# The woven SwiGLU of one encoder layer: main units in another order, and the convolution's weights transposed later

## The chip, the cores and the metric

One core of a Trainium2 chip (trn2) computes one layer of an encoder. The metric is the device time of one execution in microseconds, lower is better. Engines in this text: PE (matrix products), PEld (its weight loads), DVE and ACT (elementwise work), POOL, and SP (issues most loads).

## What is computed

All weights are float32, there are 256 rows of 2048 channels. Cut to what matters here:

```python
def _swiglu(x, w1, w3, w2):
    return (jax.nn.silu(x @ w1) * (x @ w3)) @ w2      # w1, w3: 2048 x 5632, w2: 5632 x 2048

x = _layer_norm(ALPHA * x + 0.5 * _swiglu(x, ffn1_w1, ffn1_w3, ffn1_w2), ln1_g, ln1_b)
mix = _hybrid_mixer(x, w_in, b_gates_m, conv_m, ...)  # begins with x @ w_in and a causal convolution
x = _layer_norm(ALPHA * x + mix, ln2_g, ln2_b)
x = _layer_norm(ALPHA * x + 0.5 * _swiglu(x, ffn2_w1, ffn2_w3, ffn2_w2), ln3_g, ln3_b)
x = x + jax.nn.sigmoid(x @ w_ple_gate) * (p @ w_ple_proj)
```

So there are two feed-forward networks (FFNs) of the same shape, with a mixer between them. The hidden width 5632 is 11 chunks of 512 columns, chunk 0 to 10.

## The kernel before

**Units.** The program for PE is a list of `Unit`s, written out by hand and walked from front to back (line 1043). A unit multiplies one weight tile of 256 rows by 512 columns with one half of the rows (128 rows, `tt` 0 or 1). Each float32 operand is split in two parts, hi and lo, so a unit is two k-steps of three products (lines 1061 to 1063), six in all. A weight tile is loaded on SP (line 983, `raw`), split by ACT (line 1010, hi) and by DVE (line 1014, lo), some tiles ahead of PE. Raw tiles, splits, transposed activations and wide temporaries share one pool of 44 buffers, and `loads` (line 976) issues the next load only while the count of activation buffers (`pages[0]`) and raw tiles leaves room.

**One FFN** (`ffn`, line 424) has 496 units:

- `up(c)`: for the chunks 0, 5 and 8, a gate part (x @ w1, 16 units, then Silu on ACT into a temporary `temp`) and a hidden part (x @ w3, 16 units, then a multiplication on DVE, line 442).
- `up7(c)`: for the other eight chunks gate and hidden together in a scheme of seven products (`seven`, line 314): 28 units, with sums of weights made by accumulating loads on POOL (line 330) and by DVE (line 335). Its last product is number 3; after it DVE multiplies gate and hidden for the first half of the rows (line 473), and `late` does so for the second half (line 484).
- `down(*chunks)`: the hidden chunk times w2 in four groups of 512 output columns. `down(c)` is 16 units, four for each group, two for each half; each group and half has a PSUM bank of its own, which DVE adds into the residual `xres` (line 497). `down(4, 5)` takes two chunks into one bank: 32 units with half as many additions.

Before a chunk goes into `down`, it must be transposed: `transposed` (line 263) makes four PE transposes of 128 x 128 (line 266), a copy on ACT (line 268) and a subtraction on DVE (line 274), which give the two parts of `actT` (here called hT).

**The order.** `main` is a list of parts of `up` and `down`; `chained` strings the eight `up7` chunks together (order 1, 2, 3, 4, 6, 7, 9, 10) with pauses (`None`) where a chunk waits for its sums; `weave` spreads this side list evenly over main, from main's ninth unit on. `down(9)` and `down(10)` stand behind the woven part.

**When the rest is issued.** A small planner (`Sched`) holds the steps that come later than the unit that causes them. Its clock advances by 6 x 0.2161 us a unit (line 1064), and a step is issued when it is due: a chunk is turned `DELAY["h"]` = 8 us after its multiplication, for the second half of a woven chunk `DELAY["late"]` = 9 us + 8 us after product 3, and turns are kept 3.4 us apart. If a unit needs a chunk that isn't transposed yet, the planner runs what it holds until it is:

```python
        sched.until(lambda: u.act.ready(u.chunk, u.tt))      # line 1049
```

The transposes then stand in the program right ahead of the unit that reads them.

**The convolution's weights.** `mixer_setup` (line 533) is called once, ahead of `down(9)` of the first FFN. It loads the convolution's weights (line 539) behind what SP has queued, and spawns `later` (line 547), which, 4 us on by the planner's clock, transposes them on PE (line 550) and copies them on DVE (line 551). `conv` (line 653) needs them; it follows the first group of the mixer (`head`, 16 units).

Of the kernel before, what the change touches and what calls it, by code (L numbers as in the profile page):

```python
# [156 lines left out]
def weave(main, side):  # L157

    n = sum(isinstance(u, Unit) for u in main)
    out, at, seen = [], 0, 0  # L160
    for u in main:
        out.append(u)
        if isinstance(u, Unit):
            seen += 1
            while at < len(side) and at * n < seen * len(side):
                if side[at] is not None:
                    out.append(side[at])
                at += 1
    return out


def flat(pairs):
    return [u for p in pairs for u in p]


def skewed(pairs):
    return [p[0] for p in pairs] + [p[1] for p in pairs]
# [3 lines left out]
def kernel(  # L181
# [25 lines left out]
    def temp():  # L207
        sched.until(lambda: temps[0] < TEMP_BUFS)
        temps[0] += 1
        return temp_pool.tile([P, COL], F32, name="temp", tag="temp")  # L210

    def drop(n=1):
        temps[0] -= n

    def misc(shape):
        return ps_pool.tile(shape, F32, name="ms", tag="ps")
# [19 lines left out]
    def activate(out, in_, func, **kw):  # L236
        use_table(func)
        nc.scalar.activation(out, in_, func, **kw)  # L238
# [24 lines left out]
    def transposed(src, act, c, t):  # L263
        ps = misc([P, 4, P])
        for k in range(4):
            nc.tensor.transpose(ps[:, k], src[:, k * P:(k + 1) * P], ident[:])  # L266
        dst = act.get(c, t)
        nc.scalar.copy(dst[:, 0], ps[:])  # L268
        if act.forms:
            if c not in act.whole:  # L270
                act.whole[c] = big()
                pages[0] += 1
            nc.scalar.copy(act.whole[c][:, t * COL:(t + 1) * COL], ps.rearrange("q k s -> q (k s)"))
        nc.vector.tensor_tensor(out=dst[:, 1], in0=ps[:], in1=dst[:, 0], op=ALU.subtract)  # L274
        act.mark(c, t, 4)
        if act.forms and all(act.ready(c, h) for h in range(TT)):
            sched.spawn(form_turn(act, c), DELAY["form"] + 3.0 * c)
# [26 lines left out]
    def group(w, rows, col0, cols, act, done):  # L304

        accs = [{} for _ in range(TT)]
        pairs = []
        for i, r in enumerate(rows):
            tile = plain(rows_of(w, r, col0, cols))
            pairs.append([Unit(tile, t, accs[t], act, r // COL, r % COL // P,  # L310
                               i == 0, i == len(rows) - 1, done) for t in range(TT)])
        return pairs
# [58 lines left out]
    def boundary(mixer):  # L371
        program.append(Boundary(mixer))
# [51 lines left out]
    def ffn(w1, w3, w2, act, norm, skew=True, ahead=()):  # L424
        n = FF // COL
        hT = ActT(act_tile)

        def turn(src, c, t):
            transposed(src, hT, c, t)
            drop()  # L430
            return
            yield

        def up(c):
            s = {}

            def gate(ps, t):
                s[t] = temp()
                activate(s[t][:], ps, ACT.Silu)

            def hidden(ps, t):
                nc.vector.tensor_tensor(out=s[t][:], in0=ps, in1=s[t][:], op=ALU.mult)
                sched.spaced(turn(s[t], c, t), DELAY["h"] + 2.0 * t, TURN_GAP)

            return group(w1, range(0, D, 2 * P), c * COL, COL, act, gate), group(w3, range(0, D, 2 * P), c * COL, COL, act, hidden)

        def up7(c):
            s = {}

            def both(out, a, b, op):  # L450
                nc.vector.tensor_tensor(out=out, in0=a, in1=b, op=op)

            def done(m, banks):
                ps = {k: v["ps"][:] for k, v in banks.items() if v}
                if m == 5:
                    e = temp()
                    nc.scalar.copy(e[:], ps["E"])
                    banks["B"]["ps"], banks["W"]["ps"] = seeded
                    both(banks["B"]["ps"][:], ps["X"], e[:], ALU.subtract)
                    drop()  # L460
                elif m == 6:
                    nc.scalar.copy(banks["W"]["ps"][:], ps["B"])
                elif m == 4:
                    s[1] = temp()
                    nc.scalar.copy(s[1][:], ps["E"])
                elif m == 2:
                    s[0] = temp()
                    sched.spawn(silu(s[0], ps["X"]), DELAY["silu"])
                elif m == 7:
                    both(s[1][:], ps["W"], s[1][:], ALU.add)  # L470
                    sched.spawn(silu(s[1], s[1][:]), DELAY["silu"])
                elif m == 3:
                    nc.vector.scalar_tensor_tensor(out=s[0][:], in0=ps["B"], scalar=-1.0, in1=s[0][:],
                                                   op0=ALU.mult, op1=ALU.mult)
                    sched.spaced(turn(s[0], c, 0), DELAY["h"], TURN_GAP)
                    sched.spawn(late(ps["W"]), DELAY["late"])

            def silu(out, src):
                activate(out[:], src, ACT.Silu)
                return  # L480
                yield

            def late(w):
                nc.vector.scalar_tensor_tensor(out=s[1][:], in0=w, scalar=-1.0, in1=s[1][:],
                                               op0=ALU.mult, op1=ALU.mult)
                sched.spaced(turn(s[1], c, 1), DELAY["h"], TURN_GAP)
                return
                yield

            return seven(w1, w3, D, c * COL, COL, act, done)  # L490

        def down(*chunks):
            pairs = []
            for g in range(D // COL):
                def add(ps, t, g=g):
                    xs = xres[t][:, g * COL:(g + 1) * COL]
                    nc.vector.scalar_tensor_tensor(out=xs, in0=ps, scalar=0.5, in1=xs,  # L497
                                                   op0=ALU.mult, op1=ALU.add)
                    if n - 1 in chunks:
                        norm.chunk(t, g)  # L500
                pairs += group(w2, [c * COL + r for c in chunks for r in (0, 2 * P)], g * COL, COL, hT, add)
            return pairs

        gate, hidden = zip(*(up(c) for c in (0, 5, 8)))
        program.extend((skewed(gate[0][:SKEW]) if skew else flat(gate[0][:SKEW])) + flat(gate[0][SKEW:]))
        rest, tail = down(9), down(10)
        main = flat(hidden[0] + gate[1] + down(0) + down(1) + hidden[1] + down(2) + down(3) + gate[2] + down(4, 5) + hidden[2] + down(6)
                    + down(7, 8))
        program.extend(main[:8] + weave(main[8:], chained([up7(c) for c in (1, 2, 3, 4, 6, 7, 9, 10)])))
        program.append(norm.load)  # L510
        program.extend(ahead)
        program.extend(flat(rest) + flat(tail[:-SKEW]) + skewed(tail[-SKEW:]))
        boundary(True)
# [19 lines left out]
    def mixer_setup():  # L533
        st["sel"] = big()[0:HM, 0:HM * P].rearrange("q (h s) -> q h s", s=P)
        nc.vector.memset(st["sel"], 1.0)
        nc.gpsimd.affine_select(st["sel"], st["sel"], pattern=[[-1, HM], [0, P]], compare_op=ALU.is_equal,
                                fill=0.0, base=0, channel_multiplier=1)
        raw = temp()
        nc.sync.dma_start(out=raw[0:64, 0:P], in_=conv_m[0].rearrange("j (b q) -> (j b) q", q=P))
        st["cw"] = small.tile([P, 64], F32, name="cw", bufs=1)  # L540
        st["bi"] = small.tile([HM, 1], F32, name="bi", bufs=1)
        st["bf"] = small.tile([HM, 1], F32, name="bf", bufs=1)
        bg = b_gates_m[0].rearrange("(a h) -> a h", h=HM)
        nc.sync.dma_start(out=st["bi"][:], in_=bg[0].rearrange("(h o) -> h o", o=1))
        nc.sync.dma_start(out=st["bf"][:], in_=bg[1].rearrange("(h o) -> h o", o=1))

        def later():
            yield 4.0
            ps = misc([P, 64])
            nc.tensor.transpose(ps[:], raw[0:64, 0:P], ident[0:64, 0:64])  # L550
            nc.vector.tensor_copy(out=st["cw"][:], in_=ps[:])
            drop()
            flags.add("cw")
        sched.spawn(later())
# [546 lines left out]
```

## Time and profile before

| | |
|---|---|
| three timed runs | 2250.76, 2250.98, 2256.62 us, median 2250.98 |
| the profiled execution, its own time | 2255.85 us |
| its span, first to last instruction | 2254.1 us |
| share of the span in which PE is busy | 98% |
| DVE, ACT, POOL | 75%, 55%, 9% |
| mean granted clock of PE | 0.993 |
| read from HBM | 497.91 MB, 222 GB/s over the span with what is written |

The first FFN takes the first 730 us or so, the mixer the time to about 1430 us, the second FFN the time to about 2155 us. In views of instructions a row names the line, engine and operation, then what is written and read, a count, busy us and the mean ns of one. In the waits a row says who stood idle, for whom, how long in total, how often, and the longest. A row of windows gives for each engine its busy us and in brackets the number of instructions, then the granted clock of PE (1.00 is full), the DMA engines' share and GB/s. The names in such rows are the program's: `mm` is a product's PSUM bank, `ms` the bank of a transpose, `temp` a temporary that holds a hidden chunk, `split` a split weight.

### The profile page before, as it was taken

The page shows a single profiled execution, that of the slowest core. Times are in us where ns is not written, and L with a number is a line of the kernel's source. Part 1 is how long each engine was busy: PE and PEld are TensorE (multiplying, and loading weights), DVE is VectorE, ACT ScalarE, POOL GpSimd, SP SyncE. Part 2 cuts the span into 40 slices and gives each one's busy share as a digit, 9 for nine tenths or more (in the row PEclk, how much of TensorE's full clock was granted, in tenths as well). Part 3 has the DMA queues.
Part 4 walks back from the last instruction along what each step waited for, and adds up shares of the span by engine and source line. Part 5 has one row for each costly group of instructions (what it writes and reads, how often), then busy time and mean ns, then how long its engine had stood idle before and what let it go on. Part 6 is the DMA issues. An engine that isn't in the chain of part 4 may idle for free. (4 is left out here: it accounts for less than half of the span.)

```text
span 2254.1 us, 27470 instructions
## 1 busy us (share of the span) xinstructions
PE 2213.1 (98%) x10065; PEld 1828.4 (81%) x10065; DVE 1682.6 (75%) x1840; ACT 1237.8 (55%) x1441; POOL 201.9 (9%) x175
## 2 busy tenths in 40 slices
PE   9999999999998999999999999999999999999999
PEld 7878877888887888888888888788787878888878
DVE  6889987888898765654555456788888878889873
ACT  6556655556573555545653344456565666666552
POOL 3111001011100000100100000121011110100000
PEclk9999999999999999999999999999999999999999
DMA  9899779897992665565566666679878979989542
GB/s 344 220 251 298 219 217 271 236 260 216 293 339 81 201 188 159 177 182 148 174 181 186 194 221 218 224 177 283 239 233 227 293 214 273 265 252 296 203 158 95
DMA packets 262856, 501.83 MB, mean 223 GB/s; under 512 B 15744, under 2 KB 24768, under 8 KB 262720
## 3 DMA queue, kind: packets, MB, share of 16 engines
q1 hardware_dynamic: 227904, 432.95, 58.3%
q0 software_dynamic: 34816, 67.12, 16.6%
q8 instruction: 79, 1.29, 0.2%
q14 instruction: 57, 0.47, 0.1%
HBM read 497.91 MB, written 2.10 MB: 222 GB/s over the span
## 5 line engine op out<-in xcount | busy, mean ns | idle before, releaser
L1014 DVE TENSOR_TENSOR split<-raw,split 128x1024 fp32r<-128x1024 f32 (+1 forms) x1013 | 1183.0, 1203 | 331.7 <-ACT split L1010 298.0
L1010 ACT CAST split<-raw 128x1024 fp32r<-128x1024 f32 (+1 forms) x1013 | 1018.6, 1038 | 450.6 <-PE mm L1062 104.8
L1061 PE MATMUL mm<-split,actT 128*128 128x512 f32 (+2 forms) x2768 | 1081.1, 391 | 9.3 <-ACT actT L268 8.8
L1063 PE MATMUL mm<-split,actT 128*128 128x512 f32 (+2 forms) x2768 | 1070.3, 387 | 10.6 <-DVE actT L274 10.6
L1062 PE MATMUL mm<-split,actT 128*128 128x512 f32 (+2 forms) x2768 | 1069.1, 386 | 2.6 <-DVE split L1014 2.6
L1063 PEld LDWEIGHTS mm<-split,actT 128*128 128x128 f32 x2768 | 522.7, 189 | 122.2 <-DVE actT L274 17.4
L1061 PEld LDWEIGHTS mm<-split,actT 128*128 128x128 f32 x2768 | 523.0, 189 | 112.9 <-ACT actT L268 10.7
L1062 PEld LDWEIGHTS mm<-split,actT 128*128 128x128 f32 x2768 | 523.3, 189 | 104.0 <-DVE split L1014 3.7
L330 POOL DMA_DIRECT2D raw<-in_ffn_w_dram x128 | 155.6, 1221 | 1013.2 <-DVE split L1014 823.7
L335 DVE TENSOR_TENSOR raw<-raw 128x1024 f32<-128x1024 f32 x128 | 155.7, 1217 | 11.5 <-DMA raw<-in_ffn_w_dram 11.5
L1061 PE MATMUL seeded<-split,actT 128*128 128x512 f32 x384 | 150.4, 392 | 0.0
L1063 PE MATMUL seeded<-split,actT 128*128 128x512 f32 x384 | 150.0, 391 | 0.0
L1062 PE MATMUL seeded<-split,actT 128*128 128x512 f32 x384 | 150.0, 391 | 0.0
L268 ACT CAST actT<-ms 128x512 fp32r<-128x512 f32 x84 | 49.1, 589 | 131.4 <-PE ms L266 131.2
L497 DVE SCALAR_TENSOR_TENSOR xres<-mm,xres 128x512 f32<-128x512 f32 x144 | 97.9, 683 | 21.4 <-PE mm L1063 21.4
L1061 PEld LDWEIGHTS seeded<-split,actT 128*128 128x128 f32 x384 | 72.4, 189 | 15.0
L1063 PEld LDWEIGHTS seeded<-split,actT 128*128 128x128 f32 x384 | 72.4, 188 | 15.1
L1062 PEld LDWEIGHTS seeded<-split,actT 128*128 128x128 f32 x384 | 72.4, 189 | 15.1
L274 DVE TENSOR_TENSOR actT<-ms,actT 128x512 fp32r<-128x512 f32 x84 | 57.1, 684 | 30.1 <-ACT actT L268 18.9
L421 POOL TENSOR_SCALAR xres<-xres 128x512 f32<-128x512 f32 x16 | 27.5, 1724 | 324.5 <-DVE xres L404 300.5
L238 ACT ACTIVATE temp<-mm 128x512 f32<-128x512 f32 (+1 forms) x38 | 21.8, 574 | 52.0 <-PE mm L1063 52.0
L238 ACT ACTIVATE big<-mm 128x512 f32<-128x512 f32 x20 | 12.0, 598 | 55.8 <-PE mm L1063 55.8
(124 smaller groups left out, 630.5 us busy)
## 6 DMA issues: line engine op xcount, KB each, us to landing
raw<-in_ffn_w_dram SPq DMA_DIRECT2D x527, 512.0 KB, 8.4
raw<-in_w_in_dram SPq DMA_DIRECT2D x168, 512.0 KB, 3.8
raw<-in_ffn_w_dram POOLq DMA_DIRECT2D x128, 512.0 KB, 9.5
raw<-in_w_out_dram SPq DMA_DIRECT2D x32, 512.0 KB, 4.9
raw<-in_w_ple_gate_dram SPq DMA_DIRECT2D x24, 512.0 KB, 4.9
raw<-in_w_up_m_dram SPq DMA_DIRECT2D x16, 512.0 KB, 4.1
raw<-in_w_up_sb_dram SPq DMA_DIRECT2D x16, 512.0 KB, 4.0
raw<-in_w_ple_gate_dram SPq DMA_DIRECT2D x16, 256.0 KB, 5.4
```

What stands on the lines that cost most here:

```text
L238: nc.scalar.activation(out, in_, func, **kw)
L268: nc.scalar.copy(dst[:, 0], ps[:])
L274: nc.vector.tensor_tensor(out=dst[:, 1], in0=ps[:], in1=dst[:, 0], op=ALU.subtract)
L330: nc.gpsimd.dma_start(out=raw.tile[:, :, :cols], in_=src.src, accum_op=ALU.add)
L335: nc.vector.tensor_tensor(out=a.tile[:, :, :cols], in0=a.tile[:, :, :cols], in1=b.tile[:, :, :cols], op=ALU.add)
L421: nc.gpsimd.tensor_scalar(out=xs, in0=xs, scalar1=ALPHA, scalar2=None, op0=ALU.mult)
L497: nc.vector.scalar_tensor_tensor(out=xs, in0=ps, scalar=0.5, in1=xs, op0=ALU.mult, op1=ALU.add)
L1010: nc.scalar.copy(hi[:, ks], r[:, ks])
L1014: nc.vector.tensor_tensor(out=lo[:, ks], in0=r[:, ks], in1=hi[:, ks], op=ALU.subtract)
L1061: nc.tensor.matmul(ps, hi, w[0][:, k, :u.cols], start=first, stop=False, skip_group_check=u.onto)
L1062: nc.tensor.matmul(ps, hi, w[1][:, k, :u.cols], start=False, stop=False, skip_group_check=u.onto)
L1063: nc.tensor.matmul(ps, lo, w[0][:, k, :u.cols], start=False, stop=last, skip_group_check=u.onto)
```

## The change

Main's parts stand in another order, `down(4, 5)` becomes `down(5)` and `down(4)` at two places, and the convolution's weights are transposed 12 us after `mixer_setup` instead of 4. The number of units, the side list and the weaving stay as they were.

```diff
         rest, tail = down(9), down(10)
-        main = flat(hidden[0] + gate[1] + down(0) + down(1) + hidden[1] + down(2) + down(3) + gate[2] + down(4, 5) + hidden[2] + down(6)
-                    + down(7, 8))
+        main = flat(hidden[0] + gate[1] + down(0) + hidden[1] + down(1) + down(2) + down(5) + down(3) + gate[2] + down(4)
+                    + hidden[2] + down(6) + down(7, 8))
         program.extend(main[:8] + weave(main[8:], chained([up7(c) for c in (1, 2, 3, 4, 6, 7, 9, 10)])))
...
         def later():
-            yield 4.0
+            yield 12.0
             ps = misc([P, 64])
             nc.tensor.transpose(ps[:], raw[0:64, 0:P], ident[0:64, 0:64])
             nc.vector.tensor_copy(out=st["cw"][:], in_=ps[:])
```

`gate` and `hidden` are indexed by place, so `hidden[1]` and `gate[1]` belong to chunk 5, `hidden[2]` and `gate[2]` to chunk 8.

## The prediction

> **What bounds the kernel now.** I read the page first, then the waits of PE, then the products of PE in stretches, then the waits of PE in those stretches, and last the list of units itself. From the page, the span and the engines (busy us, share, instructions):
>
> ```profile
> span 2254.1 us, 27470 instructions
> PE 2213.1 (98%) x10065; PEld 1828.4 (81%) x10065; DVE 1682.6 (75%) x1840; ACT 1237.8 (55%) x1441; POOL 201.9 (9%) x175
> ```
>
> PE carries the time: only 41 us of its span are not busy. The change doesn't remove one product, so all it can give back is time in which PE stood or ran slowly. The waits of PE (us in total, times, longest):
>
> ```profile
> PE mm L1063 <- DVE actT L274: 10.6, 11, 2.7
> PE mm L1061 <- ACT actT L268: 8.8, 8, 2.9
> PE ms L266 <- DVE temp L484: 3.5, 2, 1.8
> PE ms L550 <- DMA temp<-in_conv_m_dram: 3.1, 1, 3.1
> PE ms L266 <- DVE temp L473: 3.1, 2, 1.5
> PE mm L1062 <- DVE split L1014: 2.6, 3, 1.2
> ```
>
> L268 and L274 write the transposed activations, L473 and L484 the hidden values that L266 turns. So four of the six rows are one story, a chunk that is turned too late, and L550 is the transpose of the convolution's weights. Weights that come late (L1014) cost 2.6 us only.
>
> Where, and how much in all: a wait also drops the clock, and what a wait costs is best counted in products. The same view in windows, for the tile actT alone; (x) is the number of instructions, and every big product reads actT. The first row is a stretch without a wait, the others hold one site each:
>
> ```profile
> core 0: us, PE busy (x) PEld busy (x) DVE busy (x) ACT busy (x), PEclk, DMA share, GB/s
> 100.00:140.00 40.00, 40.00 (x178) 33.15 (x177) 0.00 (x0) 0.00 (x0) 1.00 1.01 307
> 140.00:180.00 40.00, 37.51 (x164) 30.03 (x163) 1.36 (x2) 1.17 (x2) 1.00 0.76 204
> 280.00:320.00 40.00, 34.05 (x141) 27.16 (x140) 1.38 (x2) 1.17 (x2) 0.96 0.75 200
> 380.00:420.00 40.00, 36.32 (x145) 28.65 (x144) 1.37 (x2) 1.17 (x2) 0.91 0.60 167
> 670.00:700.00 30.00, 26.21 (x102) 20.36 (x101) 0.69 (x1) 1.17 (x2) 0.89 0.50 181
> 1570.00:1600.00 30.00, 27.69 (x113) 21.72 (x112) 1.36 (x2) 1.17 (x2) 0.94 0.67 182
> 1715.00:1755.00 40.00, 34.06 (x141) 27.13 (x140) 1.38 (x2) 1.17 (x2) 0.96 0.67 171
> 1810.00:1850.00 40.00, 37.55 (x164) 30.13 (x163) 1.37 (x2) 1.17 (x2) 1.00 0.66 184
> ```
>
> 178 products in 40 us are 0.2247 us each, 1.35 us for a unit of six. Each site holds eight transposes too, which stay; the chain of waits shows a group of four:
>
> ```profile
> 1889.14 0.44 PE ms L266 x4
> ```
>
> So 0.9 us of each site is work. Lost at 140: 14 products, 3.1 - 0.9 = 2.3 us; at 280: 37, 7.4; at 380: 33, 6.5; at 670 (133.5 fit into 30 us): 31.5, 6.2; at 1570: 20.5, 3.7; at 1715: 37, 7.4; at 1810: 14, 2.3. **Together 35.8 us: 29.6 at the six sites of late chunks (16.2 in the first FFN, 13.4 in the second), 6.2 at the convolution's weights.** The lost clock is a part of it: (1 - PEclk) times the length gives 1.6 + 3.6 + 3.3 + 1.8 + 1.6 = 11.9 us.
>
> **The new order, step by step.** Which chunk belongs to which site follows from the list. An FFN is 496 units. gate 0 and the first 8 of main stand alone; then 216 main units carry 256 side entries (224 units and 32 pauses), so a woven chunk (31 entries) takes 26 main units, 54 positions. Counting in the list, the last product of the woven chunks 1, 2, 3, 4, 6, 7, 9, 10 stands at position 91, 145, 199, 253, 308, 362, 416, 463 in both orders, since main keeps its length. The down products begin at, before: chunk 1 100, 2 165, 3 200, 4 with 5 264; after: 1 133, 2 165, 5 200, 3 232, 4 299. From 331 on (hidden 8, 6, 7 with 8, 9, 10) nothing moves.
>
> The planner counts 1.297 us for a position (line 1064). It turns the first half of a woven chunk 8 us (6.2 positions) after the last product, the second half 9 + 8 us (13.1 positions) after. A down unit that comes earlier forces the turn right in front of itself, and PE waits for the whole chain. Distances before: chunk 1: 9 (second half forced), chunk 3: 1 (both), chunk 4: 11 (second half), chunk 2: 20 and chunk 10: 17 (none). The waits of PE in the windows 140:180, 280:320, 380:420 and 1570:1600 have just this shape, one chain, two, one and one:
>
> ```profile
> PE mm L1061 <- ACT actT L268: 1.2, 1, 1.2
> PE mm L1063 <- DVE actT L274: 0.6, 1, 0.6
> ...
> PE ms L266 <- DVE temp L484: 1.8, 1, 1.8
> PE ms L266 <- DVE temp L473: 1.5, 1, 1.5
> PE mm L1061 <- ACT actT L268: 1.3, 2, 0.7
> ...
> PE mm L1061 <- ACT actT L268: 2.9, 1, 2.9
> PE mm L1063 <- DVE actT L274: 0.2, 1, 0.2
> ...
> PE mm L1063 <- DVE actT L274: 0.9, 1, 0.9
> PE mm L1061 <- ACT actT L268: 0.8, 1, 0.8
> ```
>
> Distances after: chunk 1: 42, chunk 3: 33, chunk 4: 46; chunk 5 ends at 131 and is used at 200, 69. The smallest are the unmoved 17 and 20, which show no wait now; with 13.1 taken off, 33 leaves 20 positions or 27 us for transposes and copies whose waits are 0.6 to 2.9 us. So I count the 29.6 us as gone whole, waits and lost clock together. Hidden 5 comes 33 positions earlier and gate 8 32 later; their Silu on ACT and multiplications on DVE go with them, and chunk 5, done sooner, has the longest distance of all. What is late next on PE: nothing that I can find up to position 400, where a wait for weights stands that the change doesn't touch (first rival).
>
> **Added work.** Down 4 and 5 apart make 8 more additions into xres in each FFN:
>
> ```profile
> L497 DVE SCALAR_TENSOR_TENSOR xres<-mm,xres 128x512 f32<-128x512 f32 x144 | 97.9, 683 | 21.4 <-PE mm L1063 21.4
> 100.00:140.00 40.00, 40.00 (x178) 33.15 (x177) 36.28 (x36) 25.47 (x27) 6.34 (x6) 1.00 1.01 307
> ```
>
> 16 x 0.683 = 10.9 us of DVE. The second row (all tiles; third pair is DVE) is a stretch of downs 0 and 1, and DVE is busy for 36.28 of 40 us with PE full, so there is room of 9%. I count nothing; if that cover fails, at most 10.9. Products, weight loads and transposes are equal in number; SP and POOL issue the same loads in another order.
>
> **The convolution's weights.** The load is issued on SP behind a queue of weights:
>
> ```profile
> L539 SPq DMA_DIRECT2D temp<-in_conv_m_dram x1: 560/560/560, 672.4 to 672.4; - x1
> DMA to landing us min/median/max: 9.6/9.6/9.6
> ```
>
> It lands at 682.0, and PE had waited since 679.0. Due 12 instead of 4 us after setup, L550 comes 6 positions later, at 687, 5 us behind the landing. The load isn't moved; only L550 and its copy on DVE (L551) are, and both pass weight splits that no longer stand behind a wait. The first user is the conv of the head group, which ends 16 units after the FFN (position 512), the transpose being at about 474: 51 us between them. So 6.2 us go, none come.
>
> **Sum.** 35.8 us against the profiled execution, 2255.85: 2220.0. Against the median, 2250.98 (the profiled one lies 4.9 above it, as does the slowest timed run): 2215.2. If part of the 4.9 us was lost clock at these sites, the first figure is right, if it lay elsewhere, the second; I take the middle, **2217**. Two products miscounted in each of seven windows are 3.1 us, so its own range is 2212 to 2223.
>
> **Rivals.** *Weights late instead.* Turned chunks hold buffers of the common pool, and loads run only while room is left. At positions 370 to 395 six hT buffers are held (chunks 6, 7, 8), and about 20 positions on PE waits for splits:
>
> ```profile
> 585.00:625.00 40.00, 39.04 (x171) 31.69 (x170) 0.68 (x1) 0.59 (x1) 1.00 1.02 284
> 2005.00:2045.00 40.00, 38.60 (x169) 31.27 (x168) 0.68 (x1) 0.59 (x1) 1.00 1.06 298
> ```
>
> Less one group of transposes these are 1.1 and 1.6 us. In the new order chunks 1, 2 and 5 hold six from 152 to 163, a new place, but for 11 positions, not 25; before, 4, 5 and 6 held six for 13 positions (315 to 328) and no wait followed. If it comes: 2 x 1.6 and a clock drop of 1.8 each, 2224. Chance 10%.
>
> *The clock isn't cured.* If the lost clock has a cause of its own, only the waits go: 2217 + 11.9 = 2229. Against it: PEclk is below 1.00 only in windows with a wait; for it: 140, with waits of 1.2 and 0.6, keeps 1.00. Chance 6%.
> The Trainium skill ("TensorE: Matmul & The Clock Gate", HAM oscillation) puts the drop at idle gaps over about 3.4 us. No wait here is that long, so by that rule the drops wouldn't be due to the waits and this rival would hold; the rows 280 and 1715, where waits of at most 1.8 us come with 0.96, speak against it.
>
> *The clock swings in the smaller groups.* Each bank of downs 4 and 5 takes two weights in place of four, so PE changes banks twice as often there. If that lowered the clock to the least that a window above shows, 0.89, the 2 x 32 units of 1.35 us, 86 us, would take 10.7 more: 2228. Against it: 100:140 is a stretch of such groups, at 1.00 with 178 products. Chance 1%.
> The Trainium skill ("TensorE: Matmul & The Clock Gate", A second HAM failure mode: psum-queue depth-cycling) speaks for this rival: it has seen the clock oscillate where PE cycled through banks in every iteration and idled briefly between groups. By that rule the split of the down costs something; the row 100:140 doesn't bear it out.
>
> *The convolution waits anyway*, if its load now lands 5 us later against PE: 2223. The loads from position 331 on keep their places, so 4%.
>
> *Slower: DVE becomes the bound.* Downs 1, 2, 5, 3 now stand in one run, positions 133 to 263, 131 units or 177 us, in place of runs of 66. In a run each bank ends in an addition on DVE every two units, and a lag would grow from chunk to chunk, where gates let DVE catch up. To eat the gain of 34 us and 7 us more, each run must lose 21 us: DVE would have to need 198 us for 177, 112% where the row shows 91, and below 100% it loses nothing. Time: 2217 + 2 x 21 = 2259. Chance 3%.
>
> *It doesn't do what it says* (turns are still forced, by temps that run out, say): 2251. The longer held pair of gate 5 is now let go earlier, so 3%.
>
> **How the numbers follow.** Forecast 73%, weights 10, clock 6, swings 1, convolution 4, DVE 3, nothing 3. The range 2211 to 2226 holds the forecast, late weights and the convolution with their counting error; it leaves out the clock, the swings, nothing and DVE, 13%. A measurement here can tell about 0.3%, 6.8 us, from no change: the forecast and the first four rivals are faster by more, 94%; nothing is the same, 3%; DVE is slower, 3%.
>
> **What would show it.** In the new profile the rows L266 <- L473, L266 <- L484 and L550 are gone from PE's waits, L268 as well, and L274 keeps about 8 of its 10.6 us (the kernel's start and the ends of the norms); PEclk is 1.00 in both FFNs; L497 counts 160; the waits for splits stay at 2.6. Wrong would be: waits of PE for split L1014 near position 185, a DVE row near 40 of 40 in the run of downs, PEclk under 1.00 without a wait, or L550 with a wait.

## The result, and the profile after

| | before | after |
|---|---|---|
| timed runs, median | 2253.41 us (4 runs, 2250.76 to 2256.62) | 2219.06 us (4 runs, 2218.67 to 2219.43) |
| profiled execution, its own time | 2255.85 us | 2219.43 us |
| its span | 2254.1 us | 2217.6 us |

The ratio of after to before is 0.9847, 95% interval 0.983 to 0.9864: 34 us less by the medians, 36.4 us between the two profiled executions. The kernel after, run again on another chip beside other kernels (below), took 2219.07 us.

From the page of the kernel after, the span and the engines:

```profile
span 2217.6 us, 27467 instructions
PE 2198.4 (99%) x10065; PEld 1822.2 (82%) x10065; DVE 1688.1 (76%) x1856; ACT 1236.2 (56%) x1441; POOL 201.4 (9%) x175
```

The number of products is the same. PE's busy time fell as well, by 14.7 us, in the main since a product counts as busy for longer at a lower clock: in the trace of before, from 295.3 to 298.7 us at half clock, products start 0.427 us apart, against 0.227 at full clock. DVE has the 16 instructions more. Next the waits of PE, after (us in total, times, longest):

```profile
PE mm L1063 <- DVE actT L274: 8.2, 7, 2.7
PE ms L266 <- ACT split L1010: 2.2, 1, 2.2
PE mm L1062 <- DVE split L1014: 1.8, 3, 0.7
```

The rows of L473, L484, L550 and L268 (3.1, 3.5, 3.1 and 8.8 us before) are gone. What L274 keeps is the kernel's start and the ends of the norms. The second row is not new: at the same place, the norm behind the second FFN, PE waited 2.2 us before as well, put down to L407 there. L497 counts 160, at 682 ns each. The products that read actT, after, in the windows where the sites of before lay (the second FFN begins 22 us earlier now); the columns are those of before:

```profile
core 0: us, PE busy (x) PEld busy (x) DVE busy (x) ACT busy (x), PEclk, DMA share, GB/s
140.00:180.00 40.00, 39.62 (x174) 32.17 (x173) 1.37 (x2) 1.18 (x2) 1.00 0.80 226
280.00:320.00 40.00, 39.62 (x174) 32.20 (x173) 1.36 (x2) 1.16 (x2) 1.00 0.81 227
380.00:420.00 40.00, 39.81 (x176) 32.64 (x175) 0.68 (x1) 0.58 (x1) 1.00 0.82 246
660.00:690.00 30.00, 29.48 (x127) 23.36 (x127) 1.37 (x2) 1.17 (x2) 1.00 0.34 115
1540.00:1580.00 40.00, 39.62 (x174) 32.21 (x173) 1.37 (x2) 1.18 (x2) 1.00 0.80 216
1690.00:1730.00 40.00, 39.62 (x174) 32.21 (x173) 1.36 (x2) 1.16 (x2) 1.00 0.81 216
1790.00:1830.00 40.00, 40.00 (x178) 33.15 (x177) 0.68 (x1) 0.00 (x0) 1.00 0.87 253
```

174 is 178 less the place of eight transposes, which some of these windows no longer hold; 141 and 145 stood here before. PEclk is 1.00 in all of them.

The same can be had without a choice of windows. In both traces six products are one unit, so the time from the first product of one position of the list to that of another can be set side by side (us; worked out from the starts of the products):

| positions | what lies there | FFN 1 before, after | saved (forecast) | FFN 2 before, after | saved (forecast) |
|---|---|---|---|---|---|
| 98 to 133 | chunk 1 | 50.98, 48.55 | 2.4 (2.3) | 52.39, 48.55 | 3.8 (3.7) |
| 133 to 264 | chunk 3 | 188.93, 181.47 | 7.5 (7.4) | 188.91, 181.47 | 7.4 (7.4) |
| 264 to 300 | chunk 4 | 56.02, 49.43 | 6.6 (6.5) | 51.79, 49.43 | 2.4 (2.3) |
| 300 to 464 | nothing moved | 227.89, 227.86 | 0.0 | 228.38, 227.94 | 0.4 |
| 464 to 496 | convolution's weights (FFN 1) | 52.14, 46.11 | 6.0 (6.2) | 46.44, 46.43 | 0.0 |

The mixer takes 709.05 and 709.02 us. The seven sites come to 36.1 of the 36.5 us by which the spans differ.

### The profile page after: what moved, and what is told of

The parts are those of the page before. It is cut to its first block, busy times and chain, and to the rows that moved or that the text cites. A ratio compares the mean times of both kernels' runs of the same rounds, so it can differ in the third digit from the quotient of the medians.

```text
span 2217.6 us, 27467 instructions
## 1 busy us (share of the span) xinstructions
PE 2198.4 (99%) x10065; PEld 1822.2 (82%) x10065; DVE 1688.1 (76%) x1856; ACT 1236.2 (56%) x1441; POOL 201.4 (9%) x175
## 4 chain that ended last, share of the span: by engine, by line
PE 95%; DVE 3%; DMA 1%; issue 1%; ACT 0%; DVEq 0%; ACTq 0%
PE mm L1063 27%; PE mm L1062 27%; PE mm L1061 27%; PE seeded L1063 4%; PE seeded L1062 4%; PE seeded L1061 4%; PE ms L266 1%; DMA raw<-in_ffn_w_dram 1%; DVE xres L406 1%; DVE split L1014 0%; DVE xres L404 0%; DVE xres L407 0%; DVE actT L274 0%; DVE stats L391 0%; PE ms L772 0%
## 5 line engine op out<-in xcount | busy, mean ns | idle before, releaser
L497 DVE SCALAR_TENSOR_TENSOR xres<-mm,xres 128x512 f32<-128x512 f32 x160 | 108.4, 682 | 12.8 <-PE mm L1063 12.8
L268 ACT CAST actT<-ms 128x512 fp32r<-128x512 f32 x84 | 49.1, 588 | 113.8 <-PE ms L266 113.7
L1061 PEld LDWEIGHTS seeded<-split,actT 128*128 128x128 f32 x384 | 72.1, 188 | 14.7
L274 DVE TENSOR_TENSOR actT<-ms,actT 128x512 fp32r<-128x512 f32 x84 | 57.1, 684 | 30.0 <-ACT actT L268 17.7
```

Source lines behind the costliest of these rows:

```text
L1061: nc.tensor.matmul(ps, hi, w[0][:, k, :u.cols], start=first, stop=False, skip_group_check=u.onto)
```

## Experiments

The theory that these runs test: PE waits where a chunk's first reader stands closer in the list than the planner's delay, and the six late turns and the convolution's transpose add up. The rivals: the new order as such, or the split of downs 4 and 5, does it; a wait that goes is given back elsewhere; DVE is about to become the bound. Each kernel was timed beside the kernel before on the same chip (medians 2252.25, 2253.51 and 2252.27 us), the last three of the new order beside the kernel after as well.

**Order alone.** The new order with `yield 4.0` left as it was.

```diff
-            yield 12.0
+            yield 4.0
```

> The new order alone; the convolution's weights are transposed after 4 us as before. Theory of late turns: the six sites go, 29.6 us by the count of products, so about 29 to 30 us less than before, and the wait L550 <- DMA of 3.1 us stays, with its lost clock. Rival (the parts are not independent, the wait at the convolution's weights shields what is late next): the full 34 us come with the order alone, or under 25. Rival (the load of the convolution's weights is tied to PE's arrival): L550's wait is longer than 3.1 us by a good part of the 16 us that the first FFN gained.

Measured: 2223.26 us, 29.0 less; ratio 0.9875 (0.986 to 0.9891). Its wait at the convolution's weights:

```profile
PE ms L550 <- DMA temp<-in_conv_m_dram: 1.6, 1, 1.6
```

29.6 were forecast for this part. The rival of a tied load falls: the wait is shorter than the 3.1 us of before, not longer. The load landed at 663.9 us, 18 earlier than before, so it came earlier together with PE. Positions 464 to 496 take 48.08 us, 2.0 more than in the kernel after, where the old order lost 6.0: the wait is shorter and no stretch at half clock follows it, so what this site costs depends on the rest.

**Convolution alone.** The old order with the later transpose.

```diff
-            yield 4.0
+            yield 12.0
```

> The old order, only the transpose of the convolution's weights 8 us later. Theory: 6.2 us less, 3.1 of them wait, the rest lost clock and the product after it; PEclk in the stretch of that transpose rises from 0.89 to 1.00. Rival (the time is given back at the norm that ends the first FFN, where PE waits for DVE anyway): 0 to 2 us less, and the wait L1063 <- L274 behind the norm grows by as much.

Measured: 2248.12 us, 4.1 less by the medians; ratio 0.9978 (0.9969 to 0.9988), that is 2.7 to 7.0 us. The window that held 102 products before:

```profile
670.00:700.00 30.00, 29.48 (x128) 23.38 (x127) 1.38 (x2) 1.17 (x2) 1.00 0.55 201
```

128 products where 133.5 fit, and the eight transposes take the place of four: next to nothing is lost there any more. From position 464 to 496 it takes 46.11 us, 6.0 less than before, as in the kernel after. The time was not given back at the norm behind it: from there to the end of the mixer it takes 709.03 us. Order and convolution alone sum to 33.1 us, against 34.4 for both.

**The split in place.** The old order with two downs in place of one.

```diff
-gate[2] + down(4, 5) + hidden[2]
+gate[2] + down(4) + down(5) + hidden[2]
```

> The old order, with down(4, 5) as down(4) + down(5) at the same place: the 16 more additions and the smaller groups alone, chunk 4 still 11 positions behind its last product. Theory: no gain and no cost, within 1 us of before; all six sites stay. Rival (smaller groups make PE's clock swing): up to 10.7 us more. Rival (it is the split, not the distance, that frees PE): the site of chunk 4 goes, 8.8 us less.

Measured: 2253.37 us against 2252.25; ratio 1.0009 (0.9997 to 1.0021). The two sites of chunk 4 (products reading actT):

```profile
380.00:420.00 40.00, 37.44 (x156) 29.94 (x155) 1.38 (x2) 1.17 (x2) 0.96 0.63 178
1810.00:1850.00 40.00, 37.78 (x158) 30.42 (x157) 1.00 (x2) 0.58 (x1) 0.96 0.61 173
```

Both sites are there, so it isn't the split that frees PE. The 16 additions and the smaller groups cost nothing that the interval can tell, at most 4.7 us. A swinging clock of 10.7 us is outside it.

**Chunk 5 first.** The same split the other way round, which puts chunk 4 46 positions behind its last product and moves nothing but these two downs.

```diff
-gate[2] + down(4, 5) + hidden[2]
+gate[2] + down(5) + down(4) + hidden[2]
```

> The same split, but down(5) first: chunk 4 is now used 46 positions behind its last product, everything else as before. Theory of late turns: the two sites of chunk 4 go, 6.5 + 2.3 = 8.8 us less than before; the sites of chunks 1 and 3 and the convolution's weights stay. Rival (PE only waits later for something else, so a single site gives nothing): 0 to 3 us.

Measured: 2246.38 us, 5.9 less; ratio 0.9973 (0.9964 to 0.9983), 3.8 to 8.1 us. The same two sites:

```profile
380.00:420.00 40.00, 39.61 (x174) 32.19 (x173) 1.38 (x2) 1.17 (x2) 1.00 0.74 204
1800.00:1840.00 40.00, 39.62 (x175) 32.18 (x173) 1.38 (x2) 1.18 (x2) 1.00 0.74 201
```

They are clean, by 6.6 and 2.4 us in the trace, and the waits of the other sites stay. The timed gain is smaller than the 8.8 us that were expected, which lie just outside its interval. This trace doesn't say why: against the trace of before, chunk 3's site in the second FFN lost more (positions 200 to 264 took 95.61 us, before 92.87), but chunk 1's there and the convolution's weights lost 1.6 and 2.9 us less, and the span is 9.4 us shorter. How much clock a wait costs differs from run to run; the section on the hardware gives a likely reason.

**Turns planned earlier, old order.** This leaves the list alone and shortens the planner's delays.

```diff
-"ln_step": 1.7, "h": 8.0, "silu": 6.0, "late": 9.0,
+"ln_step": 1.7, "h": 4.0, "silu": 6.0, "late": 6.0,
```

> The old order and the old convolution step, but the turns planned earlier: 4 instead of 8 us after the multiplication, and the second half multiplied 6 instead of 9 us after product 3, so it is due 10 us or 7.7 positions after its chunk's last product. Theory (a turn is forced where the list's distance is shorter than the planner's delay): chunk 1 (9 positions) and chunk 4 (11) are no longer forced, chunk 3 (1) still is; the sites of chunks 1 and 4 give 2.3 + 3.7 + 6.5 + 2.3 = 14.8 us, less what is left of the wait because the turn is only 1 to 3 positions ahead of its reader: 8 to 15 us less than before. Rival (the order of the units is what counts, the delays are set so that the multiplication is done when PE comes to the turn): PE then waits at the turns of all eleven chunks for L473 and L484, 0.5 to 1.7 us each, and the time is the same or up to 20 us more.

Measured: 2240.40 us, 11.9 less; ratio 0.9945 (0.9931 to 0.9959). Chunk 4's and chunk 1's sites in the first FFN, and the waits at chunk 1's:

```profile
380.00:420.00 40.00, 39.61 (x174) 32.19 (x173) 1.37 (x2) 1.18 (x2) 1.00 0.73 201
140.00:180.00 40.00, 37.69 (x157) 30.10 (x156) 1.37 (x2) 1.17 (x2) 0.96 0.73 196
```

```profile
PE mm L1061 <- ACT actT L268: 1.0, 1, 1.0
PE mm L1063 <- DVE actT L274: 0.6, 1, 0.6
```

Chunk 4 is free of waits, chunk 3 still forced. Chunk 1 was not freed, against the expectation. The planner issues a step only between two units, so the 7.7 positions are rounded up, once at the multiplication and once at the turn: in the trace the second half of chunk 1 is transposed after position 100, right in front of its first reader at 101, exactly where it stood before. Chunk 4's second half is transposed after 262 and read at 266. So the rule needs a term more: the distance must exceed the delay, rounded up to whole units, by enough for transposes, copy and subtraction. Three units between were enough here, none was not; one and two were not tried. No waits for L473 or L484 came at other chunks, so the rival falls, and the delays were longer than they had to be.

That the 11.9 us lie in the expected 8 to 15 with chunk 1 not freed is in part luck: positions 300 to 464 also take 1.0 and 1.5 us less, since the two waits for splits at position 411 are gone (0.6 us left in all, at the kernel's start).

**The change again.** The kernel after, unaltered, on the chip of the next three kernels.

> The changed kernel once more, beside the next two. Every theory: about 34 us less than before, its times within 1 us of each other.

Measured: 2219.07 us (2218.54 to 2219.32), ratio 0.9848 (0.9831 to 0.9864).

**Turns planned later, new order.** The opposite: the kernel after, with the delay before a turn at 20 us.

```diff
-"h": 8.0
+"h": 20.0
```

> The changed kernel with turns planned 20 us instead of 8 after the multiplication, so the second half of a woven chunk is due 29 us or 22.4 positions after its last product. The order of the units is the new one. Theory of late turns (a wait stands where the distance in the list is shorter than the planner's delay): chunk 2 (20 positions) and chunk 10 (17) are now forced, four sites of one chain each, 2.3 to 3.7 us a site, 9 to 15 us more than the changed kernel; chunks 1, 3, 4, 5 (42, 33, 46, 69) stay free of waits. Rival (it is the new order as such that keeps PE fed): no forced turn and no cost, within 2 us.

Measured: 2241.47 us, 22.4 more than the 2219.07 of the kernel after on the same chip; ratio to before 0.9949 (0.9934 to 0.9963). The sites of chunk 2 and chunk 10 (windows, then the waits of PE in 2090:2110):

```profile
230.00:260.00 30.00, 27.29 (x112) 21.49 (x111) 1.37 (x2) 1.17 (x2) 0.94 0.55 173
2080.00:2110.00 30.00, 24.30 (x91) 18.71 (x90) 2.03 (x4) 1.82 (x4) 0.83 0.27 96
```

```profile
PE mm L1063 <- DVE actT L274: 2.6, 1, 2.6
PE mm L1061 <- ACT actT L268: 1.4, 2, 0.7
```

The waits came back at the two chunks that were named, in both FFNs, under the new order: the order as such feeds nothing. The size was mis-set, 22.4 us against 9 to 15. By positions chunk 2 costs 4.2 and 4.3 us, chunk 10 4.5 and 8.1, against 2.3 to 3.7 expected: at chunk 10 the first half waits too (due 15.4 positions after, rounded up to 16, so it is transposed right in front of its reader at 17), and in the second FFN the clock fell to 0.83 in 30 us there.

**Room for loads.** On top of the change, down(6) goes ahead of hidden 8 and downs 7 and 8 are apart.

```diff
-                    + hidden[2] + down(6) + down(7, 8))
+                    + down(6) + hidden[2] + down(7) + down(8))
```

> The changed kernel with down(6) ahead of hidden 8, and down(7, 8) as down(7) + down(8): chunks 6 and 8 are no longer held together, so at positions 370 to 395 two to four hT buffers are held where it were six. Theory (loads run late for want of buffers there): the waits of PE for splits at about 583 and 1986 us go, 0.7 to 1.1 us of product time each, 1 to 2 us less than the changed kernel. Rival (the burst of loads of the last two woven chunks is what is late, whatever the buffers): the waits stay, no gain; 16 more additions cost nothing.

Measured: 2217.50 us (2216.85 to 2220.73), ratio to before 0.9844 (0.983 to 0.9859); the kernel after on the same chip 2219.07 (2218.54 to 2219.32). The row of waits for splits, where the kernel after has 1.8 us:

```profile
PE mm L1062 <- DVE split L1014: 0.8, 2, 0.6
```

The waits near 583 and 1986 us are gone, and 0.6 of what is left is the kernel's start; by positions, 300 to 464 takes 1.0 and 1.1 us less, and the spans are 2216.0 and 2217.6. Whether six chunk buffers held at once were what delayed those loads stays open. The order of the loads changed here too, and the two runs with other delays speak against it: with turns planned earlier the six are held from position 372 instead of 376, and these waits are gone as well; with turns planned later they are held only from 385, and the waits are 0.8 and 1.1 us where the kernel after has 0.7 and 0.5. The 1.6 us are as expected in size, but the timed runs overlap, so that it is the fastest of all these kernels is likely, not certain.

**Twice the additions.** The kernel after, with each addition into the residual made as two of half the size.

```diff
-                    nc.vector.scalar_tensor_tensor(out=xs, in0=ps, scalar=0.5, in1=xs,
-                                                   op0=ALU.mult, op1=ALU.add)
+                    for _ in range(2):
+                        nc.vector.scalar_tensor_tensor(out=xs, in0=ps, scalar=0.25, in1=xs,
+                                                       op0=ALU.mult, op1=ALU.add)
```

> The changed kernel with every addition into the residual done as two of half the size (the same sum): 160 more instructions of 0.683 us on DVE, 109 us in all, 13 in each 54 positions of a run of downs, 8.9 of 73 us, which takes DVE from 91% to about 103% there. Theory (DVE is hidden below 100%): reserves are used up and PE waits for splits in the run from position 133 to 263, about 3% of 177 us or 5 us an FFN, at most 20 us in all, and nothing elsewhere. If DVE were still hidden there: within 2 us. If DVE were the bound already: about 100 us more.

Measured: 2247.16 us, 28.1 more than the kernel after and more than the 20 that were allowed for. Two stretches of the run of downs, all tiles (third pair DVE), first of this kernel, then of the kernel after:

```profile
240.00:280.00 40.00, 40.00 (x178) 33.15 (x177) 39.77 (x41) 24.79 (x26) 4.82 (x4) 1.00 1.00 299
320.00:360.00 40.00, 39.69 (x175) 32.45 (x174) 39.79 (x41) 23.02 (x24) 4.81 (x4) 1.00 0.98 290
```

```profile
240.00:280.00 40.00, 40.00 (x178) 33.11 (x177) 38.27 (x37) 25.28 (x26) 4.81 (x4) 1.00 1.03 310
320.00:360.00 40.00, 40.00 (x178) 33.14 (x177) 39.12 (x39) 24.86 (x26) 4.82 (x4) 1.00 1.02 308
```

With DVE busy for 39.8 of 40 us PE loses 2.4 us an FFN between positions 133 and 264, half of the 5 expected. More than half of the cost lies where the expectation had nothing: from 464 to 496, the last two downs, it takes 8.0 us more in the first FFN and 7.3 in the second. There the norm's chain on DVE follows the last additions. (The added line shifts the line numbers behind it by one: L498 is the addition here.) The waits of PE in the stretch 2080:2160 of this kernel:

```profile
PE ms L266 <- DVE xres L407: 5.7, 3, 3.0
PE ms L266 <- DVE actT L274: 1.5, 1, 1.5
PE ms L909 <- DVE xres L498: 1.2, 1, 1.2
PE mm L1062 <- DVE xres L498: 1.0, 1, 1.0
```

Of the 8.0 us in the first FFN, 1.9 are a wait put down to the copy of the convolution's weights on DVE (L552 here), at position 480. So additions in the run are nearly hidden even at that load, and the same additions are not hidden ahead of a norm.

## Why the prediction was right

2217 us was forecast with 2211 to 2226; 2219.06 came.

*The price of the sites.* Counted products gave 29.6 + 6.2 = 35.8 us; positions give 36.1 and each site within 0.2 us of its forecast. The cross-view of waits alone would have been too small: PE's waits that went sum to about 21 us (8.8 + 3.5 + 3.1 + 3.1, and 2.4 by which L274's row fell), and the rest is clock and the ends of products that the profile models.

*The list.* That chunks 1, 3 and 4 were the forced ones, and that 42, 33 and 46 positions free them, is shown from both sides: by one site freed alone, by shorter delays in the old order, and by longer delays in the new order that bring waits back at the chunks with the smallest distances. That the delay is rounded up to whole units, and that some units must stand between turn and reader, was not in the prediction. Chunk 10, the closest one left, has three: its second half is transposed after position 477 and read at 481.

*The convolution's weights.* L550 was to come 5 us behind its load. After:

```profile
L539 SPq DMA_DIRECT2D temp<-in_conv_m_dram x1: 559/559/559, 656.4 to 656.4; - x1
DMA to landing us min/median/max: 9.3/9.3/9.3
...
L550 PE MATMUL ms<-ident,temp x1: 274/274/274, 671.3 to 671.3; 64*128 64x64 f32 x1
```

It landed at 665.7 and PE read it at 671.3, 5.6 behind.

*DVE.* The additions cost nothing that shows, as was said, but the room was smaller than 9%: DVE is busy for 38.27 and 39.12 of 40 us in the run of downs, which the prediction had named as a sign against itself. The step that was off is the reading of one stretch (36.28 of 40) as the load of the whole run; the kernel before already has 39.09 of 40 in 240:280. It did no harm, since PE is full (178) in both rows, and with twice the additions it still loses only 2.4 us there.

*Weights late.* The rival did not come: the waits for splits are 1.8 us, not more than before. That held buffers cause the wait which it started from, at position 411, isn't shown; the runs with other delays speak against it.

*The clock.* The rival that the clock isn't cured falls: the half-clock stretches went with the waits. The Trainium skill ("TensorE: Matmul & The Clock Gate", HAM oscillation) asks for idle gaps of over about 3.4 us; here shorter ones do it, as the last section shows.

*Which reference.* Between 2215.2 and 2220.0 the truth lies nearer the second. The kernel before, timed again, took 2252.25 to 2253.51 by the median, 1.3 to 2.5 us over the figure that the prediction started from. The middle was taken without a reason for it, so that 2219.06 lies within about 2 us of 2217 is partly luck; the price of the sites isn't.

## What to carry to other kernels

Where an order of units is written out by hand and later steps are issued by a planner's clock, write down for each consumer its distance from the producer's last unit, and compare it with the delay, rounded up to where the planner can act, plus the chain in between; a distance that is too short shows as a wait right behind a transpose, of the same shape each time. Price such a wait by the work that is missing from a stretch of the trace, not by the wait's own length, for the clock that it costs can be as much again. What is added off the critical path should be priced by where it stands: the same additions were nearly free in the middle of an FFN and cost 7 to 8 us ahead of a norm.

## What the runs showed of the hardware

**Short waits cost clock in steps of 3.41 us.** The changes of PE's clock within a trace lie a multiple of 3.41 us apart. Cut in step with them, the stretches around chunk 3's and chunk 1's sites of the kernel before, first FFN and then second (all tiles; after POOL's pair stands PEclk):

```profile
core 0: us, PE busy (x) PEld busy (x) DVE busy (x) ACT busy (x) POOL busy (x), PEclk, DMA share, GB/s
291.85:295.27 3.42, 1.21 (x8) 0.55 (x6) 3.19 (x5) 1.46 (x4) 1.17 (x1) 1.00 1.00 192
295.27:298.68 3.41, 3.41 (x8) 2.72 (x9) 0.64 (x1) 0.86 (x1) 1.20 (x1) 0.50 0.99 253
298.68:302.09 3.41, 1.66 (x9) 1.03 (x8) 1.83 (x2) 0.00 (x0) 0.52 (x1) 1.00 1.12 233
302.09:305.51 3.42, 2.75 (x12) 1.87 (x11) 0.69 (x1) 1.45 (x2) 0.69 (x1) 1.00 1.09 177
...
1578.68:1582.09 3.41, 1.73 (x9) 0.99 (x8) 2.98 (x4) 2.28 (x3) 0.00 (x0) 1.00 1.07 297
1582.09:1585.51 3.42, 3.42 (x10) 2.66 (x9) 1.22 (x1) 1.04 (x1) 0.00 (x0) 0.50 0.19 71
```

After the first stretch, with 2.2 us of waits, the whole next one runs at 0.50, 8 products in place of 15: 1.7 us lost that no wait shows. After the third, with one long wait of 1.8 us, it doesn't; after the fifth row, with 1.7 us, it does. These two are closer than they look, as the view counts modelled ends of products: by the starts 1.92 and 2.02 us were lost. The same was done by the starts for ten of these profiles, in stretches that run at full clock themselves, counting as lost in a stretch what lies between the start of a product and the next beyond the product's own 0.227 us (a transpose's 0.11), where it exceeds 0.25 us. Of 46 stretches with 1.0 to 1.92 us lost none was followed by half clock, of 39 with 2.1 us or more all were, and of 8 in between four. With gaps counted as soon as two starts lie over 0.25 us apart, the third row and the fifth become 2.00 and 2.24 us, and all eleven profiles part without an overlap: none of 92 stretches with 1.0 to 2.09 us lost was followed by half clock, all of 48 with 2.13 us or more were. So the bound is near 2.1 us of 3.41, and by these counts what counts is how waits fall into these stretches, not the longest of them. That fits that the same site cost 2.3 us in one FFN and 3.7 in the other. It is a reading of these profiles; no run was made to vary one wait by itself.

**It may be much of the scatter.** The timed runs of the kernel before go from 2248.4 us, at a mean clock of 0.996, to 2260.0, at 0.991; 0.001 of 2250 us is 2.25 us. The kernel after, with nearly no such stretch left in its FFNs, kept its four runs within 0.8 us. That alone proves little: the run with down(6) first has as few such stretches in its trace, and its four runs spread over 3.9 us, with the clock from 0.996 to 1.000.
